# Zeros first, norm sums at fixed steps, head pairs one a step, banks ending in turn, two output blocks interleaved

## Chip, cores, metric

One core of a Trainium2 chip runs the whole program in one launch. The metric is device time in microseconds (us); the kernel before takes 1615.12 us, median of 3 runs from 1613.1 to 1617.52.

## What is computed

Two layers of a bidirectional encoder on 512 tokens of 1024 channels, all in float32. Each layer:

```python
h = _rmsnorm(x, g_mix[l])
proj = h @ w_in[l]
gate_pre, a_in, na_qkv, dil_qkv, swa_q, swa_kv = jnp.split(proj, IN_SPLITS, axis=-1)
y_a = _conformer_conv(a_in, ...)
y_b = _neighbourhood_attn(_rmsnorm(bq, na_qn[l]), _rmsnorm(bk, na_kn[l]), bv, na_rpb[l])
y_c = _dilated_attn(cq, ck, cv)
y_d = _window_gqa_sink(dq, dk, dv, swa_sink[l])
branch = jnp.einsum('bsnc,ncd->bsnd', ys, w_branch[l])
mixed = jnp.sum(jax.nn.sigmoid(gate_pre + gate_b[l]) * branch, axis=2)
x = x + mixed @ w_out[l]
x = x + _conv_ffn(_rmsnorm(x, g_ffn[l]), w_up[l], ffn_conv_w[l], ffn_conv_b[l], w_down[l])
```

The three attentions have 4 heads of 64 channels each (the windowed one 2 heads of keys and values); queries and keys are normed by head.

## The kernel before

**Products.** Activations lie transposed in SBUF, 8 tiles of 128 channels x 512 tokens. For accuracy every float32 factor is split into an upper part in a shorter format and the rest (`xh`, `xl`; `w_hi`, `w_lo`), and each product is three: upper by upper, and upper by rest both ways (`prod`, L221 to L223). One `block` is 8 channel tiles of this, 24 products, into one PSUM bank.

**Weights** are used in a fixed order, in units of 128x1024. `weights` loads a unit on SyncE's queue (`w_raw`, 2 buffers), ScalarE makes `w_hi` (L201), VectorE `w_lo` (L202), 3 buffers each. `unit` keeps two units ahead.

**The norm** is not applied to the activations. `start_norm` and `norm_tile` make `xh`, `xl` from the tile `xn` by the gains alone (L267, L268) and add up squares in `sqacc` (L276). `finish_norm` is a generator: it waits `delay` steps, sums `sqacc` over channels on TensorE with a column of ones (L290), has VectorE take the inverse root (`rstd`), puts it on diagonals (`dg`, L297), and a step later spreads it over the partitions with four more products (L302) as `RB` (L304). Results of the projections are scaled as they leave PSUM: by `rstd` where tokens lie on partitions, by `RB` where channels do.

**Order in a layer.** `token_major` computes a projection with tokens on the partitions: four banks, one for each 128 tokens, 8 k steps of 12 products (L409 to L411), a bank's result taken out (`evac`) after its last product in the eighth k step. It runs four times: Q and K of the neighbourhood attention (`project_qk`), V of two attentions (`project_v`), Q and K of the dilated attention, and Q, K, V of the windowed one (`project_swa`; Q and K leave at L517, V at L511 and L512). Then come the convolution's input (`glu`), 32 gate blocks with short branch products between them (`gates`, `branch`), 8 output blocks, 44 blocks up and 8 down in the FFN.

**Work beside the products.** The attentions, the convolution and the norm's second half are generators in `side`. `tick`, called after each k step and in each block, takes one step of each, and the scheduler places that step's instructions behind the last product so far; generators listed in `loose` are free of that. `qk_norm` belongs to them. It transposes Q and K in pairs of heads with products with the identity (L460, four a pair, into an auxiliary bank), and splits them into parts (L466 on ScalarE, L467 on VectorE). Each K half is also copied to the other 64 partitions by DMA (L476). In its first step it treats all pairs of K, in its second all pairs of Q, then it passes two steps more. The steps of `attention` follow: scores (L573, L574), mask and maximum (L587), exponential (L591), transposes of the weights (L610), values (L633, L634).

**PSUM** has eight banks, four named `mm` for projections and blocks, four named `aux` for the work beside them, each taken in turn. `update` adds a block of output to the residual and starts the next norm's tile. Each merged tile `mx` is split into `mh`, `ml` (L708, L709) for the output blocks.

**Start.** `run` sets up constants, issues the first 16 columns of parameters (L824), then eight input tiles (L829) among the first weights.

Of the kernel before, what the change touches and what calls it, by code (L numbers as in the profile page):

```python
# [14 lines left out]
F32 = mybir.dt.float32  # L15
# [7 lines left out]
P = 128  # L23
# [22 lines left out]
C_ID, C_ONE, C_DIL, C_SWA, C_COS, C_SIN = 0, 128, 136, 1032, 1416, 1480  # L46
NCST = 1544


# [128 lines left out]
class Trunk:  # L178
# [99 lines left out]
    def finish_norm(self, delay):  # L278
# [27 lines left out]

        g = work()
        self.loose.append(g)
        self.side.append(g)

# [87 lines left out]

    def token_major(self, evac):

        pss = [self.mm() for _ in range(NB)]
        mm = self.nc.tensor.matmul
        for k in range(KT):
            if k % 2 == 0:
                hi, lo = self.unit()
            s = slice((k % 2) * S, (k % 2 + 1) * S)
            for b in range(NB):
                t = slice(b * P, (b + 1) * P)
                mm(pss[b], lhsT=self.Xh[k][:, t], rhs=hi[:, s], start=k == 0, stop=False)  # L409
                mm(pss[b], lhsT=self.Xh[k][:, t], rhs=lo[:, s], start=False, stop=False)  # L410
                self.last_mm = mm(pss[b], lhsT=self.Xl[k][:, t], rhs=hi[:, s], start=False, stop=k == KT - 1)  # L411
                if k == KT - 1:
                    evac(b, pss[b])
            self.tick()

    def qk_stats(self, Q, nq, nk, rope):

# [28 lines left out]
    def qk_norm(self, Q, Qv, nq, nk, gcol):  # L446
# [21 lines left out]

        gq, gk = self.qg[:, gcol:gcol + 1], self.qg[:, gcol + 1:gcol + 2]
        for j in range(nk // 2):  # L470
            ps = pair(nq // 2 + j)
            for e, rows in enumerate(halves):
                split(ps, rows, gk[rows], KH[rows, 2 * j + e], KL[rows, 2 * j + e])
        for e, (rows, oth) in enumerate((halves, halves[::-1])):
            for t in (KH.bitcast(F32), KL.bitcast(F32)):
                nc.sync.dma_start(t[oth, e:nk:2], t[rows, e:nk:2])  # L476
        yield
        for j in range(nq // 2):
            ps = pair(j)
            for e, (rows, oth) in enumerate((halves, halves[::-1])):  # L480
                split(ps, rows, gq[rows], QS[rows, 2 * j + e], QS[oth, 2 * j + e])
        for _ in range(3):
            yield
# [35 lines left out]

    def project_qk(self, rope):  # L520
        Q = self.new_Q()
        self.token_major(self.evac_q(Q))
        return self.qk_stats(Q, 4, 4, rope)
# [188 lines left out]
    def tick(self):  # L712

        for g in list(self.side):

            with self.tc.issue_after(self.last_mm.ins) if g not in self.loose else nullcontext():
# [81 lines left out]
    def run(self):  # L798
        nc, tc = self.nc, self.tc
        with ExitStack() as st:  # L800
# [14 lines left out]
            self.w_ready = []  # L815
            self.side, self.waiting, self.head, self.loose = [], [], None, []

# [5 lines left out]
            nc.scalar.activation(warm, warm, AF.Exp)  # L823
            nc.sync.dma_start(self.prm[:, 0:16], self.PAR[0][:, 0:16])  # L824
            with tc.tile_pool(name="first", bufs=1, reuse_waits="tile") as first:
                self.start_norm('g_mix')
                for d in range(KT):
                    xn = first.tile([P, S], F32, name="xn", tag="xn", bufs=8)
                    nc.sync.dma_start(xn, self.xT[d])  # L829
                    if d == 0:  # L830
                        self.weights(1, 0, 2)
                    self.norm_tile(d, xn, first)
# [4 lines left out]
                nc.sync.dma_start(self.cst, self.CST)  # L837
                self.finish_norm(2)
            self.xres = [self.xT[d] for d in range(KT)]
# [7 lines left out]
    def layer(self, l):  # L847
        tc = self.tc
        last = l == L - 1
        self.derive_params()  # L850
        self.Y, self.mixed, self.MH, self.glu_u = [None] * 4, [], [], []
        with tc.tile_pool(name="gate", bufs=1, reuse_waits="tile") as self.gp:
            with tc.tile_pool(name="attn", bufs=1, reuse_waits="tile") as self.ap:
                self.scratch = lambda: self.gp.tile([P, S], F32, name="dg", tag="t1", bufs=2)
                late = lambda n: iter([None] * n)
                Q = self.project_qk(None)
                V = self.new_V()
                self.queue(chain(late(3), self.qk_norm(*Q, 4, 4, 0), self.attention(l, 'na', V, 1)))
                Vd = self.new_V()
# [12 lines left out]
            with tc.tile_pool(name="outp", bufs=1, reuse_waits="tile") as self.op:  # L872
                self.gates(ORDER[3])
                self.xnew = self.new_res()
                self.start_norm('g_ffn')
                for d in range(KT):
                    ps = self.mm()
                    hi, lo = self.unit()
                    for k in range(KT):
                        s = slice(k * P, (k + 1) * P)  # L880
                        self.prod(ps, hi[:, s], lo[:, s], self.MH[k][0], self.MH[k][1], k == 0, k == KT - 1)
                    self.update(d, ps, self.op, False)
                self.xres = self.xnew
                self.finish_norm(0)
        with tc.tile_pool(name="ffn", bufs=1, reuse_waits="tile") as self.fp:
# [15 lines left out]
            if not last:  # L901
                self.xres = self.xnew
                self.finish_norm(2)

# [42 lines left out]
```

## Time and profile before

| | us |
|---|---|
| median of 3 runs | 1615.12 |
| profiled execution | 1615.57 |
| its span in the trace | 1613.8 |
| outside the span | 1.77 |
| TensorE (PE) busy | 1595.9 |
| VectorE (DVE) busy | 1109.1 |
| ScalarE (ACT) busy | 779.8 |
| GpSimd (POOL) busy | 98.9 |

The profiled execution is one of the kernel's executions; its span runs from the first to the last instruction that the trace holds. "Busy" adds up the time in which an engine has an instruction at work; products on TensorE overlap, so its share says that it is hardly ever without one, not how fast they follow one another. That is read from the starts of products in the timeline. The view of waits names what an engine without work waited for last.

### The profile page before, as it was taken

The page shows a single profiled execution, that of the slowest core. Times are in us where ns is not written, and L with a number is a line of the kernel's source. Part 1 is how long each engine was busy: PE and PEld are TensorE (multiplying, and loading weights), DVE is VectorE, ACT ScalarE, POOL GpSimd, SP SyncE. Part 2 cuts the span into 40 slices and gives each one's busy share as a digit, 9 for nine tenths or more (in the row PEclk, how much of TensorE's full clock was granted, in tenths as well). Part 3 has the DMA queues.
Part 4 walks back from the last instruction along what each step waited for, and adds up shares of the span by engine and source line. Part 5 has one row for each costly group of instructions (what it writes and reads, how often), then busy time and mean ns, then how long its engine had stood idle before and what let it go on. Part 6 is the DMA issues. An engine that isn't in the chain of part 4 may idle for free.

```text
span 1613.8 us, 19874 instructions
## 1 busy us (share of the span) xinstructions
PE 1595.9 (99%) x7416; PEld 1325.8 (82%) x7416; DVE 1109.1 (69%) x1860; ACT 779.8 (48%) x1303; POOL 98.9 (6%) x168
## 2 busy tenths in 40 slices
PE   8999999999999999999999999999999999999999
PEld 6887888888888888888888878888888888888887
DVE  6678988764678778743356889887555777877321
ACT  5686766343344444432237777662434444444211
POOL 0021001221000000000000110022210000000000
PEclk9999999999999999999999999999999999999999
DMA  6532222323532333333336322223335333332342
GB/s 203 171 108 73 77 82 77 104 92 91 181 120 92 98 98 93 100 127 123 131 110 179 104 67 76 83 78 105 95 101 181 106 97 100 92 104 88 121 135 74
DMA packets 56784, 174.94 MB, mean 108 GB/s; under 512 B 6512, under 2 KB 6768, under 8 KB 56688
## 3 DMA queue, kind: packets, MB, share of 16 engines
q1 hardware_dynamic: 56688, 173.68, 34.9%
q8 instruction: 58, 0.95, 0.2%
q14 instruction: 38, 0.31, 0.1%
HBM read 157.93 MB, written 10.49 MB: 104 GB/s over the span
## 4 chain that ended last, share of the span: by engine, by line
PE 72%; DVE 1%; ACT 1%; issue 0%; POOL 0%; ACTq 0%; DVEq 0%; POOLq 0%
PE mm L221 21%; PE mm L222 21%; PE mm L223 21%; PE mm L409 2%; PE mm L411 2%; PE mm L410 2%; PE aux L610 1%; PE aux L634 1%; PE aux L573 1%; PE aux L574 0%; PE aux L633 0%; PE aux L460 0%; DVE w_lo L202 0%; PE aux L302 0%; PE aux L290 0%
## 5 line engine op out<-in xcount | busy, mean ns | idle before, releaser
L221 PE MATMUL mm<-xh,w_hi 128*128 128x512 f32 x1280 | 500.3, 391 | 3.1 <-DVE V L512 3.1
L223 PE MATMUL mm<-xh,w_lo 128*128 128x512 f32 x1280 | 498.9, 390 | 0.0
L222 PE MATMUL mm<-xl,w_hi 128*128 128x512 f32 x1280 | 498.7, 390 | 0.0
L201 ACT ACTIVATE w_hi<-w_raw 128x1024 fp32r<-128x1024 f32 (+2 forms) x273 | 284.8, 1043 | 423.9 <-PE mm L222 331.0
L202 DVE TENSOR_TENSOR w_lo<-w_raw,w_hi 128x1024 fp32r<-128x1024 f32 (+2 forms) x273 | 330.1, 1210 | 164.4 <-ACT w_hi L201 160.3
L221 PEld LDWEIGHTS mm<-xh,w_hi 128*128 128x128 f32 x1280 | 240.4, 188 | 52.8 <-DVE V L512 4.0
L223 PEld LDWEIGHTS mm<-xh,w_lo 128*128 128x128 f32 x1280 | 240.3, 188 | 50.6
L222 PEld LDWEIGHTS mm<-xl,w_hi 128*128 128x128 f32 x1280 | 240.4, 188 | 48.3
L221 PE MATMUL mm<-fh,w_hi 128*128 128x512 f32 x352 | 136.9, 389 | 0.0
L222 PE MATMUL mm<-fl,w_hi 128*128 128x512 f32 x352 | 136.9, 389 | 0.0
L223 PE MATMUL mm<-fh,w_lo 128*128 128x512 f32 x352 | 136.9, 389 | 0.0
L409 PE MATMUL mm<-w_hi,xh 128*128 128x512 f32 x256 | 102.3, 403 | 5.7 <-ACT w_hi L201 5.7
L410 PE MATMUL mm<-w_lo,xh 128*128 128x512 f32 x256 | 101.6, 397 | 0.0
L411 PE MATMUL mm<-w_hi,xl 128*128 128x512 f32 x256 | 101.6, 397 | 0.0
L344 DVE SCALAR_TENSOR_TENSOR cv<-cv,prm 128x512 f32<-128x512 f32 x120 | 94.1, 784 | 0.6
L704 POOL TENSOR_TENSOR mx<-mx,t 128x512 f32<-128x512 f32 x44 | 66.6, 1522 | 421.8 <-DVE t L703 404.0
L792 ACT ACTIVATE fh<-cy 128x512 fp32r<-128x512 f32 x44 | 27.8, 632 | 121.3 <-DVE cy L789 121.3
L746 DVE TENSOR_TENSOR xn<-mm,xr 128x512 f32<-128x512 f32 x32 | 22.1, 692 | 87.0 <-PE mm L223 78.4
L674 DVE TENSOR_TENSOR t<-mm,RB 128x512 f32<-128x512 f32 x64 | 44.0, 687 | 49.1 <-PE mm L223 48.5
L223 PEld LDWEIGHTS mm<-fh,w_lo 128*128 128x128 f32 x352 | 66.1, 188 | 13.8
L221 PEld LDWEIGHTS mm<-fh,w_hi 128*128 128x128 f32 x352 | 66.1, 188 | 13.6
L222 PEld LDWEIGHTS mm<-fl,w_hi 128*128 128x128 f32 x352 | 66.1, 188 | 13.6
(135 smaller groups left out, 2210.0 us busy)
## 6 DMA issues: line engine op xcount, KB each, us to landing
w_raw<-W SPq DMA_DIRECT2D x239, 512.0 KB, 3.6
w_raw<-W SPq DMA_DIRECT2D x32, 448.0 KB, 3.3
res<-xn SPq DMA_DIRECT2D x24, 256.0 KB, 2.0
xr<-res SPq DMA_DIRECT2D x24, 256.0 KB, 2.8
tab<-TB SPq DMA_DIRECT2D x8, 448.0 KB, 3.6
xn<-xT SPq DMA_DIRECT2D x8, 256.0 KB, 5.7
KH<-KH SPq DMA_DIRECT2D x8, 256.0 KB, 3.2
KL<-KL SPq DMA_DIRECT2D x8, 256.0 KB, 5.7
```

The lines of the kernel that those rows point to most:

```text
L201: nc.scalar.activation(hi[:, s], raw[:, s], AF.Copy)
L202: nc.vector.tensor_tensor(lo[:, s], raw[:, s], hi[:, s].bitcast(F32), ALU.subtract)
L221: mm(ps, lhsT=wh, rhs=xh, start=start, stop=False)
L222: mm(ps, lhsT=wh, rhs=xl, start=False, stop=False)
L223: self.last_mm = mm(ps, lhsT=wl, rhs=xh, start=False, stop=stop)
L344: self.after_mm(v.scalar_tensor_tensor(acc, u[:, t:t + S], w(t), acc, ALU.mult, ALU.add))
L409: mm(pss[b], lhsT=self.Xh[k][:, t], rhs=hi[:, s], start=k == 0, stop=False)
L410: mm(pss[b], lhsT=self.Xh[k][:, t], rhs=lo[:, s], start=False, stop=False)
L411: self.last_mm = mm(pss[b], lhsT=self.Xl[k][:, t], rhs=hi[:, s], start=False, stop=k == KT - 1)
L674: v.tensor_tensor(t1, ps, self.RB, ALU.mult)
L704: (v if n == ORDER[3] and d >= 6 else nc.gpsimd).tensor_tensor(m, m, t, ALU.add)
L792: nc.scalar.activation(fh, f, AF.Copy, scale=0.5)
```

## The change

It alters seven things, and no product of the computation is removed or added.

- **Zeros.** GpSimd clears a tile, and nine products of it go into an auxiliary bank that nothing reads (`WARM`).
- **First transfers.** The first input tile is issued ahead of the parameters, and the two halves of the first weight unit on ScalarE's queue.
- **Norm sums.** `finish_norm` takes an `mm` bank for the sums, its steps are placed like those of the other generators, it waits one step more before the spreading products, and the delays are 7, 1 and 1 where they were 2, 0 and 2.
- **First projection** of a layer uses `aux` banks, and its results leave after all of them are done; `derive_params` stands behind it. In layer 0 its `qk_norm` starts two steps later.
- **Banks in turn.** `token_major` runs the last two k steps bank by bank: 6 products for a bank, and then its result is taken out. A tick follows every second bank.
- **Head pairs.** For the dilated and the windowed attention `qk_norm` treats one pair in a step, and copies each K head by itself.
- **Output blocks 0 and 1** run six k steps each, and then the last two of each.

```diff
-    def weights(self, upto, ahead=3000, parts=1):
+    def weights(self, upto, ahead=3000, parts=1, queue=None):
...
-                    nc.sync.dma_start(raw[:, s], src[:, s])
+                    (queue or nc.sync).dma_start(raw[:, s], src[:, s])
...
-            ps = self.aux()
+            ps = self.mm()
...
             yield
+            yield
             ps = self.aux()
...
-        g = work()
-        self.loose.append(g)
-        self.side.append(g)
+        self.side.append(work())
...
-    def token_major(self, evac):
-
-        pss = [self.mm() for _ in range(NB)]
+    def token_major(self, evac, banks=None):
+
+        pss = [(banks or self.mm)() for _ in range(NB)]
...
-        for k in range(KT):
+
+        def prods(b, k):
...
+        for k in range(KT - 2):
             if k % 2 == 0:
                 hi, lo = self.unit()
...
+                prods(b, k)
             self.tick()
+
+        hi, lo = self.unit()
+        for b in range(NB):
+            prods(b, KT - 2)
+            prods(b, KT - 1)
+            if not banks:
+                evac(b, pss[b])
+            if b % 2 == 1:
+                self.tick()
+        if banks:
+            for b in range(NB):
+                evac(b, pss[b])
...
+        steps = [[] for _ in range(4)]
         for j in range(nk // 2):
...
+            steps[0 if gcol == 0 else j].append(('k', j))
...
         for j in range(nq // 2):
...
+            steps[1 if gcol == 0 else nk // 2 + j].append(('q', j))
+        for todo in steps:
+            for what, j in todo:
+                ps = pair(j if what == 'q' else nq // 2 + j)
...
+                    for t in (KH.bitcast(F32), KL.bitcast(F32)):
+                        nc.sync.dma_start(t[oth, h], t[rows, h])
             yield
...
-            nc.sync.dma_start(self.prm[:, 0:16], self.PAR[0][:, 0:16])
             with tc.tile_pool(name="first", bufs=1, reuse_waits="tile") as first:
+
+                z = first.tile([P, S], F32R, name="zero", tag="zero", bufs=1)
+                nc.gpsimd.memset(z.bitcast(F32), 0.0)
+                ps = self.aux()
+                for i in range(WARM):
+                    nc.tensor.matmul(ps, lhsT=z[:, :P], rhs=z, start=True, stop=True)
...
                     if d == 0:
-                        self.weights(1, 0, 2)
+                        nc.sync.dma_start(self.prm[:, 0:16], self.PAR[0][:, 0:16])
+                        self.weights(1, 0, 2, nc.scalar)
...
-                Q = self.project_qk(None)
+                Q = self.project_qk(None, self.aux)
+                self.derive_params()
...
-                self.queue(chain(late(3), self.qk_norm(*Q, 4, 4, 0), self.attention(l, 'na', V, 1)))
+                self.queue(chain(late(3 if l else 5), self.qk_norm(*Q, 4, 4, 0), self.attention(l, 'na', V, 1)))
...
+                for d in range(0, KT, 2):
+
+                    cuts = (0, KT - 2, KT) if d == 0 else (0, KT)
+                    pss, ws = [self.mm(), self.mm()], []
+                    for k0, k1 in zip(cuts, cuts[1:]):
+                        for e in range(2):
```

**TensorE at the start.** `xh` with its buffer's number is the upper part of an input tile. Before:

```order
L409 MATMUL mm<-w_hi,xh_93 128x512
L410 MATMUL mm<-w_lo,xh_93 128x512
L411 MATMUL mm<-w_hi,xl_94 128x512
L409 MATMUL mm<-w_hi,xh_93 128x512
L410 MATMUL mm<-w_lo,xh_93 128x512
```

Of the change:

```order
L849 MATMUL aux<-zero 128x512 x9
L408 MATMUL aux<-w_hi,xh_105 128x512 x4
L409 MATMUL aux<-w_lo,xh_105 128x512
L410 MATMUL aux<-w_hi,xl_106 128x512
L409 MATMUL aux<-w_lo,xh_105 128x512
```

The zeros stand first, and the four products with the upper parts alone stand ahead of those with the rests. The sums of the first norm, which stood behind 57 products of this projection, now stand behind its 96.

**TensorE between two pairs of the dilated attention, layer 0.** `L460 aux<-cst,Q` are the transposes of pairs; `cst` holds the identity. Before, with the second four of each eight from the next pair:

```order
L633 MATMUL aux<-pth,V 128x128
L634 MATMUL aux<-ptl,V 128x128
L610 MATMUL aux<-cst,e 128x128 x3
L460 MATMUL aux<-cst,Q 128x128 x8
L409 MATMUL mm<-w_hi,xh_93 128x512
L410 MATMUL mm<-w_lo,xh_93 128x512
```

Of the change, where the same step has one pair (L475 is L460 before):

```order
L652 MATMUL aux<-pth,V 128x128
L653 MATMUL aux<-ptl,V 128x128
L629 MATMUL aux<-cst,e 128x128 x3
L475 MATMUL aux<-cst,Q 128x128 x4
L408 MATMUL mm<-w_hi,xh_127 128x512
L409 MATMUL mm<-w_lo,xh_127 128x512
```

Four such groups of four now stand in four steps, 12 products apart, where two of eight stood.

**TensorE at the end of the windowed attention's projection, layer 0**, with buffer numbers; each `mm_` number is one bank. Before, the eighth k step (`xh7`):

```order
L411 MATMUL mm_1348<-w_hi_1483,xl7_168 128x512
L409 MATMUL mm_1349<-w_hi_1483,xh7_167 128x512
L410 MATMUL mm_1349<-w_lo_1484,xh7_167 128x512
L411 MATMUL mm_1349<-w_hi_1483,xl7_168 128x512
L409 MATMUL mm_1350<-w_hi_1483,xh7_167 128x512
L410 MATMUL mm_1350<-w_lo_1484,xh7_167 128x512
L411 MATMUL mm_1350<-w_hi_1483,xl7_168 128x512
L409 MATMUL mm_1351<-w_hi_1483,xh7_167 128x512
```

Of the change, two of four banks in the seventh and eighth k step, and the work between:

```order
L408 MATMUL mm_1286<-w_hi_1463,xh6_170 128x512
L409 MATMUL mm_1286<-w_lo_1464,xh6_170 128x512
L410 MATMUL mm_1286<-w_hi_1463,xl6_171 128x512
L408 MATMUL mm_1286<-w_hi_1463,xh7_179 128x512
L409 MATMUL mm_1286<-w_lo_1464,xh7_179 128x512
L410 MATMUL mm_1286<-w_hi_1463,xl7_180 128x512
L592 MATMUL aux_1559<-KH_1328,QS_1327 128x512
L593 MATMUL aux_1559<-KL_1329,QS_1327 128x512
L408 MATMUL mm_1287<-w_hi_1463,xh6_170 128x512
```

A bank's last product stood 3 products behind the last one of the bank before, and now stands 6 behind, with scores of another attention after the second bank.

## Rows read from the trace of the kernel before

**Rows 1.** The page, busy time by engine: us, share, instructions.
```profile
PE 1595.9 (99%) x7416; PEld 1325.8 (82%) x7416; DVE 1109.1 (69%) x1860; ACT 779.8 (48%) x1303; POOL 98.9 (6%) x168
```
**Rows 2.** TensorE's waits: instruction, what it waited for, us in total, times, longest.
```profile
PE mm L409 <- ACT w_hi L201: 5.7, 1, 5.7
PE mm L221 <- DVE V L512: 3.1, 2, 1.6
PE aux L460 <- DVE KL L467: 2.1, 4, 0.9
PE aux L290 <- DVE sqacc L276: 1.0, 1, 1.0
PE aux L573 <- DVE mx L587: 0.9, 2, 0.5
PE mm L221 <- ACT mh L708: 0.8, 2, 0.4
PE aux L302 <- DVE dg L297: 0.4, 2, 0.2
```
**Rows 3.** Timeline of TensorE, FFN: start, duration, instruction, idle before.
```profile
448.38 0.39 PE L221 MATMUL mm<-mh,w_hi 128*128 128x512 f32 x1
...
452.46 0.39 PE L221 MATMUL mm<-xh,w_hi 128*128 128x512 f32 x1
```
**Rows 4.** Timeline of TensorE, the start.
```profile
5.69 0.80 PE L409 MATMUL mm<-w_hi,xh 128*128 128x512 f32 x1 [5.69 <-ACT w_hi L201]
...
7.01 0.63 PE L411 MATMUL mm<-w_hi,xl 128*128 128x512 f32 x1
7.44 0.63 PE L409 MATMUL mm<-w_hi,xh 128*128 128x512 f32 x1
...
10.80 0.39 PE L411 MATMUL mm<-w_hi,xl 128*128 128x512 f32 x1
```
**Rows 5.** Timeline of all engines, the start.
```profile
0.73 0.39 SPq L824 DMA_DIRECT2D prm<-PAR  x1
...
1.18 0.42 SPq L829 DMA_DIRECT2D xn<-xT  x1
...
5.03 0.61 ACT L201 ACTIVATE w_hi<-w_raw 128x512 fp32r<-128x512 f32 x1
```
**Rows 6.** The page's groups: busy us and mean ns, idle before.
```profile
L704 POOL TENSOR_TENSOR mx<-mx,t 128x512 f32<-128x512 f32 x44 | 66.6, 1522 | 421.8 <-DVE t L703 404.0
```
**Rows 7.** Windows: us, busy by engine, then TensorE's granted clock, DMA share, GB/s.
```profile
24.00:26.00 2.00, 2.00 (x8) 1.53 (x7) 1.83 (x13) 0.00 (x0) 0.00 (x0) 0.60 0.74 203
```
**Rows 8.** Timeline of TensorE, the first norm's sums.
```profile
21.05 0.39 PE L411 MATMUL mm<-w_hi,xl 128*128 128x512 f32 x1
22.41 1.05 PE L290 MATMUL aux<-cst,sqacc 128*128 128x1 f32 x8 [0.97 <-DVE sqacc L276]
...
24.33 0.57 PE L410 MATMUL mm<-w_lo,xh 128*128 128x512 f32 x1
...
27.97 0.39 PE L410 MATMUL mm<-w_lo,xh 128*128 128x512 f32 x1
```
**Rows 9.** Timeline of TensorE, the end of output block 0, layer 0.
```profile
409.06 0.39 PE L223 MATMUL mm<-mh,w_lo 128*128 128x512 f32 x1
409.87 0.50 PE L221 MATMUL mm<-mh,w_hi 128*128 128x512 f32 x1 [0.42 <-ACT mh L708]
```
**Rows 10.** Timeline of VectorE, the FFN norm's root, from the sums to the diagonals.
```profile
453.82 0.16 DVE L293 TENSOR_SCALAR ms<-aux 128x4 f32<-128x4 f32 x1 [1.21 <-PE aux L290]
...
456.20 0.87 DVE L297 TENSOR_SCALAR dg<-cst,rstd 128x128 f32<-128x128 f32 x4
```
**Rows 11.** Timelines of ScalarE, VectorE, TensorE: first projection's scaling, last multiplication, transposes.
```profile
33.12 0.69 ACT L517 ACTIVATE Q<-mm,rstd 128x512 f32<-128x512 f32 x1 [0.80 <-PE mm L411]
...
43.34 2.50 DVE L443 TENSOR_TENSOR Q<-Q,r_y 128x512 f32<-128x512 f32 x4
...
45.94 0.82 PE L460 MATMUL aux<-cst,Q 128*128 128x128 f32 x6
```

More of the change, by code (lines that the diff above doesn't have):

```diff
@@ L7 @@
-from contextlib import ExitStack, nullcontext
+from contextlib import ExitStack
 from itertools import chain
@@ L47 @@
 NCST = 1544
+WARM = 9
 PHASE = 24
@@ L396, in y_tiles @@
         return [self.gp.tile([P, 2, S], F32R, name=n, tag=n, bufs=2) for n in ("yh", "yl")]
-    def token_major(self, evac):
-        pss = [self.mm() for _ in range(NB)]
+    def token_major(self, evac, banks=None):
+        pss = [(banks or self.mm)() for _ in range(NB)]
         mm = self.nc.tensor.matmul
-        for k in range(KT):
+        def prods(b, k):
+            t, s = slice(b * P, (b + 1) * P), slice((k % 2) * S, (k % 2 + 1) * S)
+            mm(pss[b], lhsT=self.Xh[k][:, t], rhs=hi[:, s], start=k == 0, stop=False)
+            mm(pss[b], lhsT=self.Xh[k][:, t], rhs=lo[:, s], start=False, stop=False)
+            self.last_mm = mm(pss[b], lhsT=self.Xl[k][:, t], rhs=hi[:, s], start=False, stop=k == KT - 1)
+        for k in range(KT - 2):
             if k % 2 == 0:
                 hi, lo = self.unit()
-            s = slice((k % 2) * S, (k % 2 + 1) * S)
             for b in range(NB):
[L408 to L413, printed above, removed]
-            self.tick()
+                prods(b, k)
+            self.tick()
+        hi, lo = self.unit()
[9 more added lines that the diff above has]
+                evac(b, pss[b])
     def qk_stats(self, Q, nq, nk, rope):
@@ L469, in qk_norm @@
         gq, gk = self.qg[:, gcol:gcol + 1], self.qg[:, gcol + 1:gcol + 2]
+        steps = [[] for _ in range(4)]
         for j in range(nk // 2):
[L471 to L477, printed above, removed]
-        for j in range(nq // 2):
[L479 to L482, printed above, removed]
+            steps[0 if gcol == 0 else j].append(('k', j))
+        for j in range(nq // 2):
+            steps[1 if gcol == 0 else nk // 2 + j].append(('q', j))
+        for todo in steps:
+            for what, j in todo:
+                ps = pair(j if what == 'q' else nq // 2 + j)
+                for e, (rows, oth) in enumerate((halves, halves[::-1])):
+                    h = 2 * j + e
+                    if what == 'q':
+                        split(ps, rows, gq[rows], QS[rows, h], QS[oth, h])
+                        continue
+                    split(ps, rows, gk[rows], KH[rows, h], KL[rows, h])
+                    for t in (KH.bitcast(F32), KL.bitcast(F32)):
+                        nc.sync.dma_start(t[oth, h], t[rows, h])
             yield
@@ L518, in evac_q, with project_qk @@
         return evac
-    def project_qk(self, rope):
+    def project_qk(self, rope, banks=None):
         Q = self.new_Q()
-        self.token_major(self.evac_q(Q))
+        self.token_major(self.evac_q(Q), banks)
         return self.qk_stats(Q, 4, 4, rope)
@@ L714, in tick @@
         for g in list(self.side):
-            with self.tc.issue_after(self.last_mm.ins) if g not in self.loose else nullcontext():
+            with self.tc.issue_after(self.last_mm.ins):
                 r = next(g, 'end')
@@ L815, in run @@
             self.w_ready = []
-            self.side, self.waiting, self.head, self.loose = [], [], None, []
+            self.side, self.waiting, self.head = [], [], None
             self.cst = self.const.tile([P, NCST], F32, name="cst", tag="cst", bufs=1)
@@ L837, in run @@
                 nc.sync.dma_start(self.cst, self.CST)
-                self.finish_norm(2)
+                self.finish_norm(7)
             self.xres = [self.xT[d] for d in range(KT)]
@@ L849, in layer @@
         last = l == L - 1
-        self.derive_params()
         self.Y, self.mixed, self.MH, self.glu_u = [None] * 4, [], [], []
@@ L875, in layer @@
                 self.start_norm('g_ffn')
[L876 to L882, printed above, removed]
+                for d in range(0, KT, 2):
[3 more added lines that the diff above has]
+                        for e in range(2):
+                            if k0 == 0:
+                                ws.append(self.unit())
+                            hi, lo = ws[e]
+                            for k in range(k0, k1):
+                                s = slice(k * P, (k + 1) * P)
+                                self.prod(pss[e], hi[:, s], lo[:, s], self.MH[k][0], self.MH[k][1], k == 0,
+                                          k == KT - 1)
+                            if k1 == KT:
+                                self.update(d + e, pss[e], self.op, False)
                 self.xres = self.xnew
-                self.finish_norm(0)
+                self.finish_norm(1)
         with tc.tile_pool(name="ffn", bufs=1, reuse_waits="tile") as self.fp:
@@ L902, in layer @@
                 self.xres = self.xnew
-                self.finish_norm(2)
+                self.finish_norm(1)
     def derive_params(self):
```

## The prediction

> **What bounds the kernel.** I read the engines' busy times on the page first: of a span of 1613.8 us TensorE is busy 1595.9, VectorE 1109.1, ScalarE 779.8 [rows 1]. So the bound is TensorE's list of products, and it is not shortened: the change adds nine products and removes none. What can be had is the time in which TensorE waits or runs slowly. The view of TensorE's waits lists all of that waiting [rows 2]: 5.7 us before the first product, then 3.1, 2.1, 1.0, 0.9, 0.8 and 0.4 us, 14.0 in all. The timeline gives the spacing: 18 steps from 448.38 to 452.46, so 0.227 us a product [rows 3]. Twice products come 0.43 us apart, twice as far: from the first one to 10.80 [rows 4], and from 24.33 to 27.97 [rows 8], where the granted clock reads 0.60 [rows 7]: the lower level, 1.2 GHz. In the first stretch no such reading is to be had, but the spacing is the same. The profiled execution took 1615.57 us, 0.45 over the median of 1615.12. I work against 1615.57 and take 0.45 off at the end.
>
> **The change, part by part.**
>
> *Start.* Now the first product starts at 5.69, after the weights' upper half, which ScalarE makes at 5.03, right behind its work on the first input tile [rows 4, 5]. SyncE issues that tile at 1.18, 0.45 behind the parameters at 0.73 [rows 5]. The tile is moved ahead of them: 0.45 us earlier, a first product at about 5.24. The parameters come second, 8 KB, and the weight halves leave from ScalarE's queue: the first before its table load, the second some 1 us later than now. The second is not wanted before the thirteenth product. The first four products now need the upper half of the weights alone, so the lower half, made after it, has time.
> The Trainium skill (DMA: Bandwidth & Descriptors, Issuing engines are not separate DMA queues) says that issuing from two engines saves the time of issuing only. By it the move of the weights alone brings nothing once the transfers are the limit, which no row here separates; the 0.45 is the input tile's.
> The clock: the 11 steps from 5.69 to 10.80 take 5.11 us, at 0.227 they would take 2.50: 2.61 lost [rows 3, 4]. TensorE had done nothing before 5.69, and the products became fast 5.1 us after. If products of zeros count as work, the rise comes 5.1 us after the first of them. They wait for one GpSimd memset of 128x512. No row shows one; GpSimd takes 1.52 us for an addition of that size [rows 6], the bound above; the bound below is nothing. Engines run from 0.73 on [rows 5], so zeros start between 0.8 and 2.3; I take 1.5, nearer the middle, and the rise at 6.6. Nine at 0.43 last 3.9 us, to 5.4, so they fill the time and hardly delay the first real product. Three real products stay slow, 0.6 us. Gain 2.0 from the clock and 0.45 from the tile: **2.5** (0.4 without the clock, 3.1 at most).
> The Trainium skill (TensorE: Matmul & The Clock Gate, Part 1) lets the gate follow how busy the engine is, not what its operands hold. By that rule the start brings the 2.5; no run before this one holds a product of zeros to show it.
>
> *First norm.* The sums of squares stand in the middle of the first projection and wait for the last input tile: 21.05 to 22.41 is 1.36, less 0.227: 1.13. Then nine steps from 24.33 to 27.97 take 3.64 where 2.04 would do: 1.60 [rows 8]. The change puts the sums behind all 96 products: 5.24, 0.6 and 96 times 0.227 is 27.6. What they wait for was done by 22.41. Both terms go: **2.7**. What is late next: the first projection's results. Its root now starts behind the sums, near 28.6. From the sums to the factor VectorE takes about 2.4 us [rows 10], so scaling starts near 31.0 instead of 33.12. From there to the end of the last multiplication at 45.84 it is 12.7 us now [rows 11], so 43.7 then. The transposes come 72 products and two small groups behind the sums, near 46.0. Slack 2.3, cost nothing, 2 at most.
>
> *Query and key pairs.* Waits of 2.1 us in four places are for the low part of the keys (L467) with eight transposes in a row on auxiliary banks [rows 2]. With four a step, 12 products or more lie between two pairs, 2.7 us, where the longest wait is 0.9. Gain **2.1**; half of it if VectorE is behind for other reasons. The 0.9 us on L587 stay: those scores stand ahead of the pairs as before. The pieces more, three a layer, break the chain of products: a product behind a wait lasts 0.50 instead of 0.39 [rows 9], so 0.11 for each of six, **-0.7**. SyncE gets 16 copies more, of single heads, which no product waits for now [rows 2].
>
> *Banks in turn.* 3.1 us in two places are a gate block waiting for V out of the last projection's banks [rows 2]. Now the first bank ends 9 products before the last product, then 18: 2 us more than now, against a longest wait of 1.6. Gain **3.1**, and 0.2 for two restarts: **3.3**. Below, half of it, if ScalarE's softmax work still stands ahead of the copies.
>
> *Output blocks.* The last mixed tile is late: 409.06 to 409.87 is 0.81, less 0.227: 0.58, in two layers [rows 9]. With six steps of block 1 ahead, the tile is wanted 18 products, 4.1 us, later. **1.2**.
>
> *Norm before the FFN.* 0.4 us of waits for L297, 0.6 with restarts [rows 2]. The chain gets a whole block of 24 products, 5.4 us: **0.6**. But the factor that all up-blocks need now comes behind two blocks, and one of four banks has gone to the sums. The fourth up-block needs the first one's bank: three blocks and two small groups of 1.05 [rows 8] in, 18.4 us. The first result leaves it two blocks, the groups and two copies of 0.7 in: 14.4. Nothing is lost, with 4 us to spare.
>
> Sum: 2.5 + 2.7 + 2.1 - 0.7 + 3.3 + 1.2 + 0.6 = 11.7. In layer 1 the norm's second product waits for a bank of the first projection, which is scaled only just ahead: I put 0.2 there. 1615.57 - 11.5 = 1604.1; less 0.45: **1603.6**.
>
> **Rivals.**
> 1. *Zeros do not raise the clock, or end too early.* For it: before 5.69 nothing shows what raises it. Against: it rose 5.1 us after work began. Price 2.0: 1605.6. Chance 0.12.
> 2. *The waits only move.* VectorE and ScalarE work in order, and what they make late (keys' low parts, V) may stay behind softmax work. Half of pairs and banks lost, 2.7, and 1 to 2 for the first projection's chain: 1607.3 to 1608.3. For it: the chain ended 0.1 us before its transposes in the kernel before [rows 11]. Against: each place gets more room than its wait. Chance 0.17.
> 3. *The change does not do what it says.* The scheduler might put the pieces elsewhere. The order of the changed kernel shows them at their places, so only the sizes can fail. 1612 or more, no change: 0.08.
> 4. *Slower: weights stuck behind key copies.* SyncE issues in order. A copy of the second pair now waits one step longer, some 3.3 us (12 products and a small group), and weight loads are queued behind. If a weight load were needed within that time, TensorE would wait up to 3.3 us in each of six attentions, 19.8 us, and the whole gain with it: 1603.6 + 19.8 = 1623.4. It decides from a lateness of more than the lead of the weights. Against: no wait for weights stands in the list after the first [rows 2], so they are ahead by more than nothing; how much no row tells. For one load late in each layer 6.6 us would go: 1610.2. Chance of a slower kernel 0.04.
>
> **How the numbers follow.** Forecast 0.59: 1603.6, on its own 1600.5 to 1606. The low end is all bounds taken kindly (start 3.1, restarts saved, L587's 0.9 gone): some 3 us more than the sum. The high end takes rival 1 and 2 in and part of rival 4: 1610. About 0.3%, 4.8 us, is what a measurement of this kernel can tell from no change; faster needs under 1610.3. The forecast and rivals 1 and 2 are that: 0.88; rival 3 is no change, 0.08; rival 4, 0.04.
>
> **What would show it.** First product near 5.2 with zeros ahead of it, and spacings of 0.227 from about 6.6 on; a rise near 10 would be rival 1. No gap near 21 and no clock under 1.00 near 25. L467's successor, V's and mh's gone from the list of TensorE's waits, mx's still in it. Weights in that list, or transposes of Q waiting near 46, would be rivals 4 and 2. I am wrong if under 8 us are won, or if over 15 are.

## Result: 1605.96 us, 10 less than before

The changed kernel takes 1605.96 us, the median of 6 runs (1604.57 to 1606.45), beside 1615.93 for the kernel before on the same chips. The ratio is 0.9938, with a 95% interval from 0.9925 to 0.9951. Forecast were 1603.6, in a range from 1600.5 to 1610. So the sign and the rough size were right. The sum held because misses of opposite sign met, which is in part luck; two of its terms were far off, as the runs show.

The profiled execution's span is 1604.1 us, 9.7 less than before. The page's busy times hardly moved, as for [rows 1]:

```profile
PE 1594.7 (99%) x7425; PEld 1328.0 (83%) x7425; DVE 1110.1 (69%) x1860; ACT 778.6 (49%) x1303; POOL 99.9 (6%) x169
```

TensorE's waits in the changed kernel, with the columns of [rows 2]:

```profile
PE aux L592 <- DVE yf L659: 1.6, 2, 0.8
PE aux L849 <- POOL zero L846: 1.3, 1, 1.3
PE aux L408 <- ACT w_hi L204: 1.2, 1, 1.2
PE aux L592 <- DVE ptl L636: 0.6, 1, 0.6
PE aux L592 <- DVE mx L606: 0.5, 1, 0.5
PE mm L408 <- DVE V L531: 0.2, 1, 0.2
```

Gone are V at the gates, the keys' low parts, `sqacc`, `mh` and `dg`. New are yf (scores that want an auxiliary bank which VectorE hasn't emptied), ptl (the same, for a bank of transposes), and a wait for weights of 1.2 us behind the zeros. The start in TensorE's timeline, to be held against [rows 4]:

```profile
1.30 4.21 PE L849 MATMUL aux<-zero 128*128 128x512 f32 x9 [1.30 <-POOL zero L846]
6.67 2.08 PE L408 MATMUL aux<-w_hi,xh 128*128 128x512 f32 x4 [1.16 <-ACT w_hi L204]
8.55 0.63 PE L409 MATMUL aux<-w_lo,xh 128*128 128x512 f32 x1
...
10.62 0.39 PE L410 MATMUL aux<-w_hi,xl 128*128 128x512 f32 x1
10.85 0.39 PE L409 MATMUL aux<-w_lo,xh 128*128 128x512 f32 x1
```

The first real product is not 0.45 us earlier but 0.98 later, and products come 0.43 us apart until 10.3, nearly as before. And on the other engines, to be held against [rows 5]:

```profile
0.73 0.41 ACTq L201 DMA_DIRECT2D w_raw<-W  x1
0.73 0.38 SPq L853 DMA_DIRECT2D xn<-xT  x1
1.18 0.42 SPq L855 DMA_DIRECT2D prm<-PAR  x1
...
4.86 0.72 ACT L270 ACTIVATE xh<-xn,prm 128x512 fp32r<-128x512 f32 x1 [2.20 <-DMA prm<-PAR]
```

ScalarE's first work on the input starts at 4.86; before, it started at 3.88. What [rows 8] showed is gone: the last product ahead of the sums starts at 30.14, and the sums follow without a wait.

```profile
30.14 0.39 PE L410 MATMUL aux<-w_hi,xl 128*128 128x512 f32 x1
30.37 0.95 PE L293 MATMUL mm<-cst,sqacc 128*128 128x1 f32 x8
31.18 0.49 PE L408 MATMUL mm<-w_hi,xh 128*128 128x512 f32 x1
```

From here on the start of those sums serves as a mark: all 96 products of the first projection lie ahead of it, and differences in the span can be split there.

### The profile page after: what moved, and what is told of

The parts are those of the page before. It is cut to its first block, busy times and chain, and to the rows that moved or that the text cites. A ratio compares the mean times of both kernels' runs of the same rounds, so it can differ in the third digit from the quotient of the medians.

```text
span 1604.1 us, 19934 instructions
## 1 busy us (share of the span) xinstructions
PE 1594.7 (99%) x7425; PEld 1328.0 (83%) x7425; DVE 1110.1 (69%) x1860; ACT 778.6 (49%) x1303; POOL 99.9 (6%) x169
## 4 chain that ended last, share of the span: by engine, by line
PE 92%; DVE 4%; ACT 2%; issue 1%; DMA 0%; SPq 0%; ACTq 0%; DVEq 0%
PE mm L224 25%; PE mm L226 25%; PE mm L225 25%; PE mm L408 2%; PE mm L410 2%; PE mm L409 2%; PE aux L629 1%; DVE w_lo L205 1%; PE aux L408 1%; PE aux L409 1%; PE aux L410 1%; PE aux L653 1%; PE aux L592 1%; PE aux L652 1%; PE aux L593 1%
## 5 line engine op out<-in xcount | busy, mean ns | idle before, releaser
L408 PE MATMUL mm<-w_hi,xh 128*128 128x512 f32 x192 | 76.4, 398 | 0.3 <-DVE V L531 0.2
L410 PE MATMUL mm<-w_hi,xl 128*128 128x512 f32 x192 | 75.1, 391 | 0.0
L409 PE MATMUL mm<-w_lo,xh 128*128 128x512 f32 x192 | 74.9, 390 | 0.0
```

## Experiments

### 1. The start: what came late, and what raises the clock

Four variants of the changed kernel. The first puts the parameters ahead again:

```diff
+                nc.sync.dma_start(self.prm[:, 0:16], self.PAR[0][:, 0:16])
                 self.start_norm('g_mix')
...
                     if d == 0:
-                        nc.sync.dma_start(self.prm[:, 0:16], self.PAR[0][:, 0:16])
                         self.weights(1, 0, 2, nc.scalar)
```

> The changed kernel with the first 16 parameter columns issued ahead of the first input tile again; all else as changed. In the changed kernel the first real product started at 6.67 us, because the parameters issued second landed at 4.8 (ScalarE's first input work at 4.86 waited for them). If that order is the cause of the late start: first real product at 5.0 to 5.5 us. On the clock, three theories. A, products of zeros count as work and only the gap of 1.2 us between zeros and products kept the clock down: here zeros run into the products, products 0.23 us apart from about 6.4 on, sums of the first norm near 27.5 instead of 30.4. B, zeros count for nothing: 0.23 apart from about 10.3, sums near 29.2. C, the rise comes at about 10.5 whatever is done before: sums near 29.3. If the order is not the cause: first product still near 6.7.

It took 1606.06 us, the span 1604.3. The expectation fell: the first real product came at 6.94, later still. Now the input tile is what ScalarE waits for:

```profile
5.65 0.72 ACT L270 ACTIVATE xh<-xn,prm 128x512 fp32r<-128x512 f32 x1 [2.98 <-DMA xn<-xT]
```

That tile was issued at 1.18 us, as in the kernel before, where the work on it began at 3.88. So the order of the two is not the cause; whichever is second lands late. The sums began at 30.32 and decide nothing on the clock, since the gap behind the zeros had grown to 1.4 us.

The second variant drops the zeros and their memset.

> The changed kernel without the nine products of zeros and their memset; all else as changed. First real product as changed, about 6.7 us. If zeros bring the rise of the clock forward in part (it came 3.8 us after the first real product, 5.1 in the kernel before): products 0.23 us apart from about 11.8, and the whole 0.7 us longer than the changed kernel. If they do nothing: from about 10.5 as changed, and the same time.

It took 1606.11 us. The first real product came at 6.85, products were 0.27 apart or less from 10.30 on, and the sums began at 30.55, against 30.37. In the profiled execution of the changed kernel the nine zeros thus bought 0.2 us at most. The fast products began between 10.1 and 10.8 in this run, in the first variant, in the changed kernel and in the kernel before, for first real products from 5.69 to 6.94; the delay of 5.1 us that the forecast took from one row is not a constant (here, without zeros, it is 3.5).

The third has 16 zeros (`WARM = 16`), so that TensorE has no gap.

> The changed kernel with 16 products of zeros instead of 9, so that TensorE has no gap ahead of the first real product. A (zeros count, the gap kept the clock down): zeros become 0.23 apart near 6.4, end near 7.3, all real products 0.23 apart, sums of the first norm near 29.1 instead of 30.4. B (zeros count for nothing): zeros 0.43 apart to 8.1, products slow until 13.2, sums near 32.5. C (rise at about 10.5 whatever comes before): zeros to 8.1, products slow until 10.5, sums near 31.2.

It took 1606.00 us. Theory A holds: the zeros became fast on their way, every real product was fast, and the sums began at 29.07. That this meets the expected 29.1 to the tenth is chance: the first product came 0.5 earlier than expected, and 0.4 was lost behind it, waiting for the lower part of the weights, `w_lo`.

```profile
1.31 5.66 PE L849 MATMUL aux<-zero 128*128 128x512 f32 x16 [1.31 <-POOL zero L846]
6.80 0.40 PE L408 MATMUL aux<-w_hi,xh 128*128 128x512 f32 x1
```

Sixteen zeros from 1.31 to 6.80 are 5.49 us, where 0.43 each would be 6.9 and 0.227 each 3.6. In the trace the first nine start 0.43 us or more apart, up to 4.89, and those from 5.18 on 0.24 or less, so the rise came near 5. But the span is that of the changed kernel. The 1.3 us went again before 101 us: TensorE has two new waits, 0.2 us at 84.5 and 0.7 at 89.5, both at scores of the first attention, and the wait that ends at 101.1 ends at the same time as in the changed kernel. More on this stretch under 3.

The fourth has the parameters first and 11 zeros.

> Parameters first again, and 11 products of zeros, so that the zeros reach into the time of the first real product. A: first real product near 6.0, products 0.23 apart from about 6.4, sums of the first norm near 27.9. B: products slow until about 11, sums near 30. C: slow until about 10.5, sums near 29.9. If A holds, this is no better than 9 zeros with the parameters first.

It took 1604.16 us, 1.9 less than the first variant with nine. The first real product came at 6.68, 0.5 behind the zeros, all were fast, and the sums began at 28.60. On the clock that fits A and excludes B and C, though the first product did not come near 6.0; here the gain was kept to the end (span 1602.4).

### 2. The start: whose transfers were in the way

The same with the first weights on SyncE's queue again, as in the kernel before:

```diff
-                        self.weights(1, 0, 2, nc.scalar)
+                        self.weights(1, 0, 2)
```

> Transfers at the start as in the kernel before (parameters, first input tile, both halves of the first weights, all on SyncE's queue), with 11 products of zeros; the rest as changed. Theory: the first input tile and the parameters landed late (ScalarE's first input work at 4.86, 5.65 and 5.38 us in the changed kernel and two variants, 3.88 before) because the weights issued at 0.73 and 1.23 from ScalarE's queue share the transfer engines with them. Then: ScalarE's first input work near 3.9, first real product near 5.7, products 0.23 us apart from the start, sums of the first norm near 27.7 (28.6 with the weights on ScalarE's queue), the whole near 1603.2. Rival, that the late landing has another cause (the profiled run's transfers, the order of the first input work): first real product still near 6.7 and sums near 28.6.

It took 1602.96 us. ScalarE's first work is back near 3.9 and the zeros run into the real products:

```profile
3.99 0.72 ACT L270 ACTIVATE xh<-xn,prm 128x512 fp32r<-128x512 f32 x1 [1.76 <-DMA xn<-xT]
```
```profile
1.30 5.04 PE L849 MATMUL aux<-zero 128*128 128x512 f32 x11 [1.30 <-POOL zero L846]
6.17 1.11 PE L408 MATMUL aux<-w_hi,xh 128*128 128x512 f32 x4
7.11 0.39 PE L409 MATMUL aux<-w_lo,xh 128*128 128x512 f32 x1
...
27.99 0.95 PE L293 MATMUL mm<-cst,sqacc 128*128 128x1 f32 x8
```

The sums begin 2.4 us ahead of the changed kernel's, and the span is 2.9 shorter. The fourth variant differs from this one by the queue of the weights alone, so that queue was the cause of the late start. The transfers themselves show it: from its issue the first tile takes 2.6 us to land in the kernel before, 3.6 in the changed kernel and 2.7 here, the 8 KB of parameters 1.7, 3.6 and 1.8. That they share the DMA engines with the 256 KB halves is the reading of these times. Both this variant and the same with nine zeros were then timed.

> The variant with the transfers of the start on SyncE's queue and 11 zeros, timed. One look gave 1602.96. If the early rise of the clock holds in every execution: median 1602.5 to 1603.5, all executions within 1 us of each other, 3 us below the changed kernel's 1605.96. If it holds in some only: some of them near 1605.

> The same with the nine zeros of the change. In the changed kernel nine zeros end at about 5.5 us and the first real product comes 1.2 later; in the profile the clock rose only at 10.5, in the variant with the output blocks apart it rose early in spite of a gap of 1.5. Here the real products come 0.2 to 0.5 us behind the zeros. If the gap is what kept the clock down: products 0.23 us apart from the start in every execution, median as with 11 zeros or up to 0.4 us lower. If nine are too few by themselves: in some executions products 0.43 apart to about 10, sums of the first norm near 29.5, and times spread over 1.5 us or more.

With 11 zeros: 1603.51 us, median of 5 (1602.91 to 1603.88), ratio to the kernel before 0.9930, interval 0.9916 to 0.9943. With nine: 1603.23 (1603.13 to 1603.55), ratio 0.9930, interval 0.9917 to 0.9942. With nine the first real product came soon behind the zeros, and all were fast:

```profile
1.31 4.21 PE L849 MATMUL aux<-zero 128*128 128x512 f32 x9 [1.31 <-POOL zero L846]
5.91 1.18 PE L408 MATMUL aux<-w_hi,xh 128*128 128x512 f32 x4 [0.39 <-ACT w_hi L204]
```

The sums began at 28.16. This variant differs from the first one by the queue alone, and its five times lie within 0.5 us; so nine were enough where the products followed soon. Both versions take some 2.5 us less than the changed kernel's 1605.96, and no run of either reaches that kernel's lowest, 1604.57. The times alone do not settle it: here the kernel before took 1613.86 (1613.05 to 1618.66), 2.1 less than beside the changed kernel, and the intervals of the ratios overlap. The traces do: with nine zeros the span is 2.8 us shorter than the changed kernel's, and 2.2 of it lie ahead of the sums.

In the changed kernel, with 1.2 us between zeros and products, it is open from one execution to the next: its spans were 1604.1 to 1604.7 in five of six runs, and 1602.8 in one. Two variants below with the same start show what went with an early rise. In the one with output block 1 apart all real products were fast, 1.5 us behind the zeros; in the one with the banks together four were, 1.8 behind them, and those from 7.96 to 10.95 slow. In these two the nine zeros took less than the 4.21 us of the changed kernel:

```profile
1.30 3.96 PE L849 MATMUL aux<-zero 128*128 128x512 f32 x9 [1.30 <-POOL zero L846]
```
```profile
1.31 3.75 PE L839 MATMUL aux<-zero 128*128 128x512 f32 x9 [1.31 <-POOL zero L836]
```

So their clock had risen while zeros still ran, at 4.8 and 4.4 us. With 11 zeros it rose anywhere from 4.2 to 6.6, without a change in when the zeros began (1.3). The changed kernel's nine zeros, while slow, end at 5.5, so that a rise falls inside them in some executions only; where it had not come by then and a gap of 1.2 us or more followed, it came only at 10.1 to 10.6.

### 3. Banks in turn

`token_major` as before, all four banks in each k step; the first projection still in auxiliary banks.

```diff
-        for k in range(KT - 2):
+        for k in range(KT):
             if k % 2 == 0:
                 hi, lo = self.unit()
...
+                if k == KT - 1 and not banks:
+                    evac(b, pss[b])
             self.tick()
...
-        hi, lo = self.unit()
-        for b in range(NB):
-            prods(b, KT - 2)
-            prods(b, KT - 1)
-            if not banks:
-                evac(b, pss[b])
-            if b % 2 == 1:
-                self.tick()
```

> The changed kernel with the projections' last two k steps in the old order (all four banks in each k step, a tick after each); the first projection still in auxiliary banks. Theory: a gate block waits for V again, about 1.6 us in each layer, 3.4 with restarts. The changed kernel has two new waits of 0.8 us for yf on VectorE (at 100 and 947 us) and one of 0.6 for ptl. If they come from results leaving their banks earlier and crowding VectorE, those at 100 and 947 go: net 1.5 us slower than the changed kernel. If they come from elsewhere they stay: net 3.4 slower.

It took 1615.43 us: not 1.5 to 3.4 slower, but 9.5, all that the change had won. The sums began at 30.36, as in the changed kernel, so all of it lies behind them. TensorE's waits:

```profile
PE mm L411 <- DVE V L521: 3.7, 1, 3.7
PE mm L224 <- DVE V L521: 3.4, 2, 3.0
...
PE aux L582 <- DVE ptl L626: 1.6, 3, 0.8
```

The wait of 3.7 us, from 55.9 on, has no counterpart in the kernel before. There the next projection began on V's banks without a wait. With the sums behind the whole first projection, and the first `qk_norm` two steps later for it, the split of keys and queries comes on VectorE just when V should leave its banks: from 51.0 to 57.4 its timeline has four key splits of 2.9 us together, four query splits of 3.0 together, and one piece of V between them. In the kernel before the same splits were done by 54.2, and V left from 57.3 on. The wait of 3.0 us, in layer 1, ends at 949.04, that of 1.5 in the kernel before at 948.98: TensorE came earlier, V did not. And the waits of 3.0 and 3.7 have a second price. The clock falls behind them; the windows, with the columns of [rows 7]:

```profile
58.00:60.00 2.00, 0.37 (x1) 0.40 (x2) 2.00 (x4) 1.33 (x4) 0.00 (x0) 0.75 0.31 79
60.00:62.00 2.00, 2.00 (x6) 1.52 (x6) 1.54 (x4) 0.86 (x2) 0.00 (x0) 0.50 0.93 247
...
950.00:952.00 2.00, 2.00 (x7) 1.54 (x6) 1.84 (x4) 2.00 (x7) 0.00 (x0) 0.50 0.00 0
```

So the part that takes the banks in turn is worth more in the changed kernel than the 3.3 us that the waits of the kernel before showed. By these timelines it also pays for the late sums, and in layer 1 it keeps what other parts have won. No run has the banks together and the sums early in the changed kernel, so how much falls to each stays open.

One of the new waits, in the changed kernel at 100 us, is read from the chain of waits of the stretch from 97 to 101.3:

```profile
96.91 1.29 DVE Q L458 x2
98.20 1.14 DVE w_lo L205
99.33 0.60 DVE Q L458
99.94 0.07 DVE rl L616
100.01 0.59 DVE t L330
100.60 0.03 issue
100.63 0.43 DVE yf L659
101.06 0.04 issue
101.10 0.39 PE aux L592
```

yf, on which TensorE waits, stands behind the multiplication of the next queries, a weight split and the convolution's input. With the banks together this wait is still there, 0.8 us at 104.9, so results that leave earlier are not its cause; the one at 947 is gone, and two more for ptl are there. One more run asked whether it is a chance meeting: the best variant with the first attention of layer 0 one step later (`late(3 if l else 6)`).

> The variant with the transfers on SyncE's queue and 11 zeros, with the first attention's work in layer 0 starting one step (12 products, 2.7 us) later. Its wait for yf at 97.7 us came because VectorE had a weight split and a multiplication of the next projection's queries (1.9 us) in its queue ahead of yf. If it is that meeting, one step later moves it: the wait at 98 goes or changes by more than 0.3, 0.7 us are won. If VectorE is simply too full in that stretch: it stays as it is. No wait elsewhere is expected to change in layer 1.

It took 1605.37 us, 2.4 more than without that step; 0.3 of it lie ahead of the sums, where nothing was changed. The wait near 97 fell from 0.5 to 0.3 and is for ptl now, new ones of 0.7 and 0.8 came at 153.6 and 159.1, and one of 0.6 at 271 became three small ones up to 282:

```profile
PE aux L592 <- DVE yf L659: 1.8, 3, 0.8
...
PE aux L592 <- DVE ptl L636: 1.3, 3, 0.7
```

So this shift moved waits rather than ending them; other shifts were not tried.

### 4. Pairs, one a step

`qk_norm` as before:

```diff
-        steps = [[] for _ in range(4)]
         for j in range(nk // 2):
...
+            ps = pair(nq // 2 + j)
...
+                nc.sync.dma_start(t[oth, e:nk:2], t[rows, e:nk:2])
+        yield
         for j in range(nq // 2):
+            ps = pair(j)
```

> The changed kernel with all pairs of K in one step and all pairs of Q in the next, and their copies together, as before; the rest as changed. Theory: four waits of transposes for the low part of keys return, 2.1 us, 2.8 with restarts. The wait at 100 us for yf lies ahead of the dilated attention's pairs and stays; the one at 947, if it comes from the pairs' place among the auxiliary banks, goes. Net 2 to 2.8 us slower than the changed kernel.

It took 1606.96 us, the span 1605.1, 1.0 more than the changed kernel. Three of four waits for keys return:

```profile
PE aux L475 <- DVE KL L482: 2.4, 3, 0.9
...
PE aux L589 <- DVE yf L656: 0.9, 1, 0.9
```

They cost 3.0 us with restarts. But the waits for mx at 905 and for yf at 947 are gone, 1.6 with theirs, and a small one at 957, 0.2. Pairs one a step are worth 1 us, since more than half of what they win comes back as waits in layer 1.

### 5. Output blocks apart

```diff
-                    cuts = (0, KT - 2, KT) if d == 0 else (0, KT)
+                    cuts = (0, KT)
```

> The changed kernel with output block 1 behind all of block 0; the rest as changed. Theory: the wait for mh returns, 0.4 us in each layer, 0.6 with the product's own spacing, and the restarts for ml behind it 0.4 more: 1.9 in all, and nothing else moves. If the mixed tiles come earlier in the changed kernel: less.

It took 1606.19 us, the span 1604.4. The wait is back:

```profile
PE mm L224 <- ACT mh L727: 0.9, 2, 0.4
```

The span is only 0.3 over the changed kernel's, but in this execution the clock rose early: sums at 28.66 instead of 30.37. Behind that mark it is 0.3 + 1.7 = 2.0 us longer, near the 1.9 expected. A difference of two totals would have called this part nearly worthless.

### 6. Zeros alone

The kernel before with 11 zeros and nothing else:

```diff
+                z = first.tile([P, S], F32R, name="zero", tag="zero", bufs=1)
+                nc.gpsimd.memset(z.bitcast(F32), 0.0)
+                ps = self.aux()
+                for i in range(11):
+                    nc.tensor.matmul(ps, lhsT=z[:, :P], rhs=z, start=True, stop=True)
                 self.start_norm('g_mix')
```

> The kernel before with nothing changed but 11 products of zeros ahead of the first real product. In the changed kernel with these 11 zeros every real product was 0.23 us apart, and the sums of the first norm stood behind all 96 products. Here they stay in the middle of the first projection and wait for the last input tile, which the zeros do not bring sooner (done at about 22.4). Theory: the clock's gain of about 2.2 us is given back at once, as a wait for sqacc of about 3 instead of 1.0 us, sums still at 22.4, and slow products behind them as before; the whole within 0.5 us of the kernel before. Rival: the gains add, and the kernel is 2 to 2.6 us faster.

It took 1612.06 us, beside one run of 1617.69 for the kernel before; the span is 1610.3, 3.5 less than the 1613.8 of that kernel's profile. Both sides of the expectation fell, the theory by all of it. The scheduler placed the sums eight products later than without zeros, so that the wait for the tile did not grow, and behind it the clock did not fall:

```profile
20.84 0.39 PE L410 MATMUL mm<-w_lo,xh 128*128 128x512 f32 x1
22.11 1.05 PE L290 MATMUL aux<-cst,sqacc 128*128 128x1 f32 x8 [0.89 <-DVE sqacc L276]
```
```profile
24.00:26.00 2.00, 2.00 (x10) 1.62 (x9) 1.22 (x9) 1.06 (x1) 0.00 (x0) 1.00 0.85 236
```

The same kind of wait, 0.9 us and then the sums, brought the clock to 0.60 in [rows 7] and leaves it at 1.00 here. So 1.6 us of what the forecast gave to the place of the sums can also be had without moving them, at least in this execution.

## Why the prediction held, and where it did not

*Start, forecast 2.5: the step failed.* "The tile is moved ahead of them: 0.45 us earlier, a first product at about 5.24." It came at 6.67. The forecast moved the tile on its queue and left the transfers themselves as they were; but the weights, put on a second queue, now ran beside tile and parameters, which took 3.6 us each to land. It expected the second half some 1 us later than before; both halves were issued earlier, at 0.73 and 1.23 where it was from 1.65 on, and that was priced at nothing. Product 13 started at 11.04 before and at 11.31 in the changed kernel: 0.3 lost where 2.5 were forecast. The page of the Trainium skill that the forecast cited (DMA: Bandwidth & Descriptors, Issuing engines are not separate DMA queues) says that transfers from several issuers interleave on the same engines. The trace agrees: first input work at 3.88, 3.99 and 4.09 us with one issuer, from 4.86 to 5.65 with two. The forecast took from the page what is saved, and not what interleaving can cost the tile.

*Clock.* The mechanism was right: in the runs with 11 and 16 zeros real products ran at the higher level from the first or second one on. The rule cited from the Trainium skill (TensorE: Matmul & The Clock Gate, Part 1), that the clock follows how busy the engine is, agrees with that. What was missing was the gap: "Nine at 0.43 last 3.9 us, to 5.4, so they fill the time" rested on the first product at 5.24. And the rise, taken as 5.1 us behind the first zero from one row, came 2.9 to 5.3 us behind it in the runs where it came early. Rival 1, with its second half ("or end too early"), took place in the profiled execution.

*First norm, forecast 2.7:* wait and slow stretch are both gone. The slack of the first projection's chain was forecast as 2.3 us. In the changed kernel its last multiplication ended at 46.14 + 1.89 = 48.03, and the transposes began at 48.55, with 0.5 to spare; rows that answer to the last two of [rows 11]:

```profile
46.14 1.89 DVE L458 TENSOR_TENSOR Q<-Q,r_y 128x512 f32<-128x512 f32 x3
```
```profile
48.55 1.03 PE L475 MATMUL aux<-cst,Q 128*128 128x128 f32 x8
```

Weight splits stood between on VectorE. It held, by less than thought. What it did not see is that everything behind the late sums comes later on VectorE as well.

*Banks, forecast 3.3:* the waits for V at the gates are gone, and undone in the changed kernel this part costs 9.6 of the span. As a reading of the kernel before 3.3 was right; as a part of the whole it was far too small.

*Pairs, forecast 2.1 - 0.7 = 1.4:* 1.0 measured. The four waits went, and what was taken off for restarts came as waits for banks. "The 0.9 us on L587 stay" was half right: 0.5 is left, in layer 1; why the one in layer 0 went was not tested.

*Output blocks, forecast 1.2:* 2.0, since the restarts for `ml` behind the wait were left out. *Norm before the FFN, 0.6:* the wait for `dg` is gone, and no wait for a bank took its place.

*Rival 2* took place in part: yf and ptl, 2.2 us in three waits, are work of VectorE and ScalarE that stands ahead in their queues. *Rivals 3 and 4* did not: every part stands where the order showed it, and no product waits for weights after the first.

So -2.8 at the start and -2.2 in new waits stand against +0.8 for the blocks and, as a remainder, some +2.4: restarts that went with the waits for keys (0.7), a wait for mx that went in layer 0 (0.6), and restarts charged to the change that are not to be seen. That leaves 9.7 of the span where 11.5 were forecast. The remainder was not measured part by part, and that misses of 5.0 one way met 3.2 the other is luck. The low end of the range, "some 3 us more than the sum", adds up to 2.2 from the terms that it names.

## What to carry to other kernels

Where two parts of a change move work on the same helper engine, their prices do not add: undo each in the changed kernel as well, and split the result at a mark in the timeline, since a difference of totals hides a part behind another's luck. A transfer on a second queue is not a transfer earlier; ask whose bytes it runs beside, above all in the first microseconds. Work that only warms the clock has to last until the clock has risen and run into the real work, so first measure when the real work starts, and the rise in more than one execution.

## What the runs showed of the hardware

The clock's rise is not a fixed time behind the first product. Without an early rise fast products began at 10.1 to 10.8 us in five kernels whose first real product stood anywhere from 5.69 to 6.94. With zeros from 1.3 us on it rose between 4.2 and 6.6 us in nine executions; in three more, whose nine zeros ended slow at 5.5 with 1.2 to 1.4 us of gap behind them, it rose at 10.1 to 10.6. Once up, it stayed up over gaps of 0.3 to 0.5 us and one of 1.5. It fell about 1 us after the end of a gap of 1.8. A wait of 3.0 and one of 3.7 us brought it down for some 3.4 us; one of 1.0 before the sums did in one kernel, and one of 0.9 in another did not.

An addition of 128x1 on VectorE lasts 0.16 us in the median, and 1.25 where GpSimd adds 128x512 at the same time; that addition lasts 2.20 where the median is 1.30:

```profile
271.69 1.25 DVE L614 TENSOR_TENSOR ls<-ls,sk 128x1 f32<-128x1 f32 x1
```
```profile
270.72 2.20 POOL L723 TENSOR_TENSOR mx<-mx,t 128x512 f32<-128x512 f32 x1 [7.77 <-DVE t L722]
```

All of the six such additions over 0.4 us in the kernel before and all eight in the changed one begin during an addition of GpSimd and end about 0.02 us behind it; no other addition of that kind meets one. The one shown stands ahead of ptl, for which TensorE waits 0.6 us at 273.6. No run took GpSimd's additions away, so that the one holds up the other is read from their places and not shown.
